# Gate and branch projections moved between the steps of a delta rule, and later DMA landings in a kernel's own planner

## The chip, the core and the metric

The kernel runs on one core of a Trainium2 chip. Its time is device microseconds of one execution, the median of several runs; less is better.

## What is computed

A sequence of 256 tokens with 1024 channels goes through two attention layers, a norm, and then twice through a "mixer" and a feed-forward network. The change lies in the mixer. Cut to what matters:

```
def hybrid_mixer(h, w_in, ...):
    proj = h @ w_in                       # 1024 x 7688
    (dn_qkv, dn_z, dn_b, dn_a, ret_q, ret_k, ret_v, ret_g, pool_u, gates) = split(proj)
    q, k, v = split(silu(causal_depthwise_conv(dn_qkv, dn_conv)))   # 4 taps, 4 heads of 128
    o_dn   = gated_delta_rule(l2(q), l2(k), v, sigmoid(dn_b), g)    # chunks of 64 tokens
    o_pool = multiscale_pool(pool_u, pool_w, pool_scale)
    o_ret  = chunkwise_retention(rotary(ret_q), rotary(ret_k), ret_v, ...)
    gt = sigmoid(gates).reshape(b, s, 3, 1024)
    y = (gt[:, :, 0] * (o_dn   @ w_branch_dn)
       + gt[:, :, 1] * (o_pool @ w_branch_pool)
       + gt[:, :, 2] * (o_ret  @ w_branch_ret))
    return y @ w_out
```

Inside the delta rule each chunk solves a triangular system (I + M) with M from k, the gates beta and the decays; the result feeds a state that is carried over four chunks of 64 tokens.

## The kernel before

Weights are read in float32. `piece` (two 128-row blocks of a weight matrix, up to 512 columns) issues one DMA into a `raw` tile on SP's queue, lets ScalarE cast it to `whi` and VectorE form the remainder `wlo`; there are 4 `raw`, 7 `whi` and 7 `wlo` buffers. `dense` then makes three matmuls for each block and each half of the tokens (whi and wlo against the two parts of the activations), into one of three `acc` PSUM tiles. So a product of 1024 x 512 weights is 4 pieces and 48 matmuls of 512 columns, one of 512 x 512 weights is 2 pieces and 24 matmuls.

A mixer (`mixer`) is written in this order. Retention comes first (its q, k, v and gate projections, its scores and its output `oT[4:8]`), then the pool (`oT[0:4]`), then `z0` (the delta rule's z, beta and a columns). From a come, in some twenty VectorE operations on 128x8 tiles, the log-decays `gg`; TensorE multiplies `gg` with four masks. Then come the decay masks `em` and `emT`, and `qkv(1, kTr)`: 96 matmuls of 256 columns and, on VectorE, two multiplications by `rr`, twelve convolution taps and two silu operations. Then M and `kn`, the solve of the 16x16 diagonal blocks (cN is moved by eight 8 KB DMAs to `Nb`, thirty small VectorE operations on `Tb`, eight DMAs back to `cT`), then `Tm` and `Sm`, `qkv(2, vT)`, `level(4)`, `qkv(0, qT)`, `level(5)`, the state over the four chunks, the normalised output `oTd`. Only behind all this stand, in the text, `gate` (the gates' columns, 1024 x 512 at a time, a tanh into a `tg` tile) and `branch` (512 x 512 at a time, its result times 1 + `tg` into `y`): pool in two halves, retention in two halves, then both gate halves of the delta rule, its branches and `w_out`.

The text's order is not the order on the engines. `Prog.record` writes down every operation with a cost and a priority (its place in the text), and `schedule` plays a machine through: each engine takes, of the operations that are ready, the one with the lowest place, and buffers of a class are handed out in the order of the text. What comes out is the fixed order of each engine's instructions; on the chip each engine then runs its list in order. When a DMA lands in this model is set by two lines:

```
hw = max(hw, t) + 460
dma = max(dma, hw + 840) + a.free() * a.shape[0] * 4 / 350.0
o.end = dma + 700
```

with a cost of 600 for loads that are broadcast over the partitions (`pv`, `gains`) and 380 for all others. `pv` (one buffer) holds small parameters; the mixer's first operation on VectorE halves 640 columns of it in place (`nrm`). Since `pv` comes free when the mixer before has used it last, the second mixer's `pv` is loaded, and halved, in the middle of the first mixer. In the trace every operation has line 389, the line of `emit` that issues it; tiles tell them apart (`b` and `s` are shared by many arrays, `m` and `ty` are the 128x8 ones, `kk` the constants, `st` the state).

Of the kernel before, what the change touches and what calls it, by code (L numbers as in the profile page):

```python
# [12 lines left out]
AF = mybir.ActivationFunctionType  # L13
ALU = mybir.AluOpType
AX = mybir.AxisListType

P = 128
S = 256
D = 1024
# [202 lines left out]
class Prog:  # L222
# [78 lines left out]
    def schedule(self):  # L301
        import heapq
        queue = {c: list(reversed(t)) for c, t in self.tiles.items()}
        free = {c: [(0.0, s) for s in range(v[0])] for c, v in self.classes.items()}
        waiting = {}
        for o in self.ops:
            o.wait += len(o.vts)
            for vt in o.vts:
                waiting.setdefault(id(vt), []).append(o)
        engines = ("PE", "DVE", "ACT", "POOL", "SP")  # L310
        now = {e: 0.0 for e in engines}
        pend = {e: [] for e in engines}
        avail = {e: [] for e in engines}
        dma = hw = 0.0
        held = {"DVE": 0.0, "POOL": 0.0}

        def release(o, t):
            o.ready = max(o.ready, t)
            o.wait -= 1
            if o.wait == 0:  # L320
                heapq.heappush(pend[o.eng], (o.ready, o.pri, id(o), o))

        def assign(c):
            while free[c] and queue[c]:
                vt = queue[c].pop()
                t, vt.slot = heapq.heappop(free[c])
                vt.avail = t
                for o in waiting.pop(id(vt), []):
                    release(o, t)
                if vt.left == 0:  # L330
                    heapq.heappush(free[c], (t, vt.slot))

        for c in self.classes:
            assign(c)
        order = []
        while len(order) < len(self.ops):
            best = None
            for e in engines:
                if avail[e] or pend[e]:
                    t = now[e] if avail[e] else max(now[e], pend[e][0][0])  # L340
                    if best is None or t < best[0]:
                        best = (t, e)
            if best is None:
                raise RuntimeError("the schedule is stuck: a class has too few slots")
            t, e = best
            while pend[e] and pend[e][0][0] <= t:
                _, p, i, o = heapq.heappop(pend[e])
                heapq.heappush(avail[e], (p, i, o))
            o = avail[e][0][2]
            if e in ("DVE", "ACT") and not o.crit:  # L350
                c = [q for q in pend[e] if q[3].crit and q[0] < t + 0.8 * o.cost and q[1] < o.pri]
                if c:
                    now[e] = min(c)[0]
                    continue
            heapq.heappop(avail[e])
            if self.shared(o):
                t = max(t, held["POOL" if e == "DVE" else "DVE"])
                held[e] = t + o.cost
            o.start = t
            now[e] = t + o.cost  # L360
            o.end = now[e]
            if e == "SP":
                a = (o.outs + o.ins)[0]
                hw = max(hw, t) + 460
                dma = max(dma, hw + 840) + a.free() * a.shape[0] * 4 / 350.0
                o.end = dma + 700
            order.append(o)
            for q in o.succ:
                release(q, o.end + LAT.get((e, q.eng), 100))
            for vt in o.vts:  # L370
                vt.left -= 1
                vt.last = max(vt.last, o.end)
                if vt.left == 0:
                    heapq.heappush(free[vt.cls], (vt.last + (230 if e == "PE" else 150), vt.slot))
                    assign(vt.cls)
        self.order = order
        self.span = max(o.end for o in order)
# [14 lines left out]
class Net:  # L392
# [541 lines left out]
    def mixer(self, l, xT, rx, nxt):  # L934
        nc = self.nc
# [2 lines left out]
        conv = pp[:, 0:48].rearrange("p (c k) -> p c k", k=4)  # L938
        psc, pw = pp[:, 48:52], pp[:, 52:564].rearrange("p (g d) -> p g d", g=4)
        nrm = pv[:, 8:648]  # L940
        nc.vector.tensor_scalar(nrm, nrm, 0.5, None, ALU.mult)
        dnn, retn = nrm[:, 0:128], nrm[:, 128:640]
        W = lambda *cols: self.chunk("w_in_2", l, list(cols))
        ts = lambda tt: slice(tt * P, tt * P + P)
        oT = self.new_xT()

        def plain(cols, fn):
            p = W(*cols)
            for tt in range(2):
                a = self.acc([P, sum(c[1] - c[0] for c in cols)])  # L950
                self.dense(a, xT, tt, p)
                fn(tt, a)
# [13 lines left out]
        def rot(tt, ps, dst):  # L966
            nat = self.s2([P, 4, P])
            self.rope(nat, ps.rearrange("p (h d) -> p h d", h=4), self.cosR, self.sinR, 4, P, tt, nc.vector, rx[tt][:, 0:1])
            pt = self.sd([P, 4, P])
            self.transposes(pt, nat.rearrange("p h d -> p (h d)"), 4)  # L970
            nc.scalar.copy(dst[:, :, ts(tt)], pt)
# [12 lines left out]
        a0 = self.acc([P, 512])  # L984
        self.dense(a0, xT, 1, pk)
        rot(1, a0, rkT)
        sc0 = self.b(9, [P, 4, S])
        sc1 = self.b(10, [P, 4, P])
        for h0 in (0, 2):
# [15 lines left out]
        for tt in range(2):  # L1005
# [14 lines left out]
            o = self.s2([P, 4, P])  # L1020
# [48 lines left out]
        a = sm()  # L1069
# [110 lines left out]
        kt = self.b(1, [P, 2, 4, P])  # L1180
        for tt in range(2):
            nc.vector.tensor_tensor(kt[:, tt], kn[:, tt], hd(tail, tt), ALU.mult)
        cp = self.b(0, [P, 832])
        cN, cT = (cp[:, i * P:i * P + P].rearrange("p (t h c) -> p t h c", t=2, h=4) for i in range(2))
        Nb, Tb = (cp[0:64, 320 + i * 256:576 + i * 256].rearrange("p (r c) -> p r c", r=16) for i in range(2))
# [13 lines left out]
        for tt in range(2):  # L1199
            for h in range(4):  # L1200
                nc.sync.dma_start(cT[:, tt, h], Tb[(tt * 4 + h) * 8:(tt * 4 + h) * 8 + 8])
        y = [self.b(12 + tt, [P, D]) for tt in range(2)]
        Tm, Sm = self.b(8, [P, 2, 4, P]), self.b(9, [P, 2, 4, P])
        for tt in range(2):
            nc.vector.tensor_tensor(Tm[:, tt].rearrange("p h (b c) -> p h b c", c=16),
# [5 lines left out]
        def level(lv):  # L1211
            for tt in range(2):
                ps = self.sd([P, 4, P])
                for h in range(4):
                    nc.tensor.matmul(ps[:, h], M[:, tt, h], Sm[:, tt, h], start=True, stop=True)
                wt = self.s2([P, 4, P])
                nc.vector.tensor_tensor(wt, ps, self.hb(self.masks[lv]), ALU.mult)
                ps = self.sd([P, 4, P])
                for h in range(4):
                    nc.tensor.matmul(ps[:, h], Tm[:, tt, h], wt[:, h], start=True, stop=True)  # L1220
                nc.vector.tensor_tensor(Sm[:, tt], Sm[:, tt], ps, ALU.subtract)
                if lv < 5:
                    nc.vector.transpose(Tm[:, tt].rearrange("p h d -> p (h d)"), Sm[:, tt].rearrange("p h d -> p (h d)"))

        qkv(2, vT)
        vb = self.b(5, [P, 2, 4, P])
        for tt in range(2):
# [2 lines left out]
        kb = self.b(2, [P, 2, 4, P])  # L1230
        for tt in range(2):
            nc.vector.tensor_tensor(kb[:, tt], kn[:, tt], hd(bGr, tt), ALU.mult)
        level(4)
        qkv(0, qT)
        rqs = []
# [4 lines left out]
        for tt in range(2):  # L1240
# [2 lines left out]
                nc.tensor.matmul(ps[:, h], kTr[:, h, ts(tt)], qT[:, h, ts(tt)], start=True, stop=True)  # L1243
            nc.vector.tensor_tensor(attnT[:, tt], ps, emT[:, tt], ALU.mult)
        level(5)
        uu, wq0, wq1 = self.b(10, [P, 2, 4, P]), self.b(3, [P, 4, P]), self.b(3, [P, 2, 4, P])
        wq = {(0, 1): wq0, (1, 0): wq1[:, 0], (1, 1): wq1[:, 1]}
        for tt in range(2):
# [12 lines left out]
        o = self.b(4, [P, 2, 4, P])  # L1261
# [41 lines left out]
            self.transposes(pt, of, 4)  # L1303
            self.split(oTd[0][:, :, ts(tt)], oTd[1][:, :, ts(tt)], pt)

        def gate(bi, h):
            tg = []

            def fn(tt, a):
                t = nc.tile("tg", [P, 512])  # L1310
                nc.scalar.activation(t, a, AF.Tanh, scale=rx[tt][:, 1:2])
                tg.append(t)
            plain([(4616 + bi * D + h * 512, 4616 + bi * D + h * 512 + 512)], fn)
            return tg

        def branch(name, h, src, k0, tg, first):
            s = slice(h * 512, h * 512 + 512)
            p = self.chunk(name, l, [(h * 512, h * 512 + 512)], 4)
            for tt in range(2):
                a = self.acc([P, 512])  # L1320
                self.dense(a, src, tt, p, k0)
                if first:
                    nc.vector.scalar_tensor_tensor(y[tt][:, s], tg[tt], 1.0, a, ALU.add, ALU.mult)
                else:
                    nc.vector.scalar_tensor_tensor(tg[tt], tg[tt], 1.0, a, ALU.add, ALU.mult)
                    nc.vector.tensor_tensor(y[tt][:, s], y[tt][:, s], tg[tt], ALU.add)

        for h in range(2):
            branch("w_branch_pool_2", h, oT, 0, gate(1, h), True)
        for h in range(2):  # L1330
            branch("w_branch_ret_2", h, oT, 4, gate(2, h), False)
        tgs = [gate(0, h) for h in range(2)]
        yT = self.new_xT()
        for h in range(2):
# [146 lines left out]
```

## Time and profile before

| | us |
|---|---|
| median of 3 runs (1206.88 to 1207.74) | 1206.95 |
| profiled execution, its own time | 1212.46 |
| its span, first to last instruction | 1210.7 |
| TensorE busy in the span | 1182.1 |
| mean granted TensorE clock | 0.993 of full speed |

The profile adds up busy time per engine; an engine's idle time before an instruction is listed with what ended it. "PE" is TensorE, "DVE" VectorE, "ACT" ScalarE, "SPq" the queue that issues the DMAs. Mixer 0 ends some way into the span (about 230 to 545 us), mixer 1 runs from about 725 to 1015 us; their delta rules begin near 334 and 808 us.

### The profile page before, as it was taken

The numbers are of one execution on the slowest core, as the hardware profiler recorded it, in microseconds if no ns is written. First come the engines' busy times: TensorE is split into PE (matmuls) and PEld (weight loads), VectorE is DVE, ScalarE is ACT, GpSimd is POOL, SyncE is SP. The second block draws the span as 40 slices with busy tenths as digits, with TensorE's granted clock in tenths as the row PEclk, the third lists the DMA queues.
The fourth block names the chain that finished last, engine by engine and source line by source line (L and its number), as shares of the span: only waits on it lengthen the run. The fifth ranks groups of instructions, "written<-read, shape, count | busy, mean of one in ns | idle before, by whom it ended". The sixth has DMA issues, their size and how long they took to land.

```text
span 1210.7 us, 17627 instructions
## 1 busy us (share of the span) xinstructions
PE 1182.1 (98%) x6468; PEld 1002.0 (83%) x6468; DVE 878.7 (73%) x1584; ACT 644.1 (53%) x1196; POOL 48.4 (4%) x65
## 2 busy tenths in 40 slices
PE   8999999999989999999999999999899999999997
PEld 6898889888889788887888888899788888788886
DVE  7988789887679877677655638679977866655643
ACT  6687568855345444555544536445454545544431
POOL 0100110000001001000000001000000001000000
PEclk9999999999989999999999999999999999999999
DMA  7354435545461763546554864544374454664661
GB/s 252 111 162 118 144 106 191 182 147 176 123 203 54 214 216 105 174 124 219 170 184 134 266 208 139 166 136 153 111 241 136 143 192 126 205 206 135 203 204 36
DMA packets 64664, 197.10 MB, mean 163 GB/s; under 512 B 11200, under 2 KB 12608, under 8 KB 64576
## 3 DMA queue, kind: packets, MB, share of 16 engines
q1 hardware_dynamic: 64576, 195.96, 50.3%
q8 instruction: 51, 0.84, 0.3%
q14 instruction: 37, 0.30, 0.1%
HBM read 194.62 MB, written 1.05 MB: 162 GB/s over the span
## 4 chain that ended last, share of the span: by engine, by line
PE 80%; DVE 10%; DMA 5%; ACT 3%; issue 2%; POOL 0%; SPq 0%; POOLq 0%; ACTq 0%; DVEq 0%
PE acc L389 63%; PE sd L389 17%; DVE s L389 3%; DMA raw<-in_wt 3%; DVE wlo L389 3%; DVE b L389 2%; ACT whi L389 1%; DMA pv<-in_pv 1%; ACT b L389 1%; DMA raw<-in_wc 1%; DVE ty L389 1%; POOL ty L389 0%; DVE tg L389 0%; DMA gc<-in_gcol 0%; SPq L389 0%
## 5 line engine op out<-in xcount | busy, mean ns | idle before, releaser
L389 DVE TENSOR_TENSOR wlo<-raw,whi 128x1024 fp32r<-128x1024 f32 (+4 forms) x380 | 428.7, 1136 | 145.7 <-ACT whi L389 143.4
L389 ACT CAST whi<-raw 128x1024 fp32r<-128x1024 f32 (+4 forms) x380 | 370.3, 982 | 237.8 <-PE acc L389 144.5
L389 PE MATMUL acc<-whi,xh 128*128 128x512 f32 (+4 forms) x1184 | 446.2, 378 | 5.7 <-ACT whi L389 2.4
L389 PE MATMUL acc<-wlo,xh 128*128 128x512 f32 (+4 forms) x1184 | 444.2, 376 | 6.0 <-DVE wlo L389 6.0
L389 PE MATMUL acc<-whi,xl 128*128 128x512 f32 (+4 forms) x1184 | 444.3, 376 | 0.0
L389 PEld LDWEIGHTS acc<-wlo,xh 128*128 128x128 f32 x1184 | 223.7, 189 | 46.4 <-DVE wlo L389 8.4
L389 PEld LDWEIGHTS acc<-whi,xh 128*128 128x128 f32 x1184 | 223.1, 189 | 45.8 <-ACT whi L389 3.5
L389 PEld LDWEIGHTS acc<-whi,xl 128*128 128x128 f32 x1184 | 223.6, 189 | 37.7 <-DVE xl L389 0.3
L389 PE MATMUL acc<-whi,b 128*128 128x512 f32 x328 | 107.1, 396 | 0.0
L389 PE MATMUL sd<-b,b 128*128 128x128 f32 (+3 forms) x496 | 74.8, 291 | 0.3 <-ACT b L389 0.2
L389 PEld LDWEIGHTS acc<-whi,b 128*128 128x128 f32 x328 | 61.5, 188 | 14.1
L389 PEld LDWEIGHTS sd<-b,b 128*128 128x128 f32 (+2 forms) x496 | 65.1, 191 | 6.5 <-DVE b L389 2.0
L389 POOL TENSOR_TENSOR ty<-ty,m 128x4 f32<-128x4 f32 (+3 forms) x34 | 33.7, 993 | 878.5 <-DVE ty L389 878.5
L389 PE MATMUL acc<-wlo,b 128*128 128x512 f32 x164 | 64.7, 395 | 0.0
L389 ACT ACTIVATE b<-sd 128x512 fp32r<-128x512 f32 (+3 forms) x44 | 23.4, 537 | 60.1 <-PE sd L389 57.9
L389 PE MATMUL acc<-xh,wlo 128*128 128x256 f32 x192 | 55.1, 287 | 0.0
L389 PE MATMUL acc<-xh,whi 128*128 128x256 f32 x192 | 54.7, 286 | 0.0
L389 PE MATMUL acc<-xl,whi 128*128 128x256 f32 x192 | 54.6, 285 | 0.0
L389 ACT ACTIVATE s<-acc,r 128x512 f32<-128x512 f32 (+3 forms) x52 | 31.2, 600 | 43.1 <-PE acc L389 40.3
L389 PE MATMUL sd<-c,s 128*128 128x128 f32 (+2 forms) x260 | 40.1, 274 | 1.7 <-DVE s L389 1.5
L389 DVE SCALAR_TENSOR_TENSOR b<-sd,b 128x512 fp32r<-128x512 f32 (+3 forms) x44 | 26.7, 615 | 18.1 <-ACT b L389 17.2
L389 PEld LDWEIGHTS sd<-c,s 128*128 128x128 f32 (+2 forms) x260 | 30.7, 138 | 9.8 <-DVE s L389 3.2
(172 smaller groups left out, 1274.7 us busy)
## 6 DMA issues: line engine op xcount, KB each, us to landing
raw<-in_wt SPq DMA_DIRECT2D x308, 512.0 KB
raw<-in_wt SPq DMA_DIRECT2D x40, 256.0 KB
raw<-in_wt SPq DMA_DIRECT2D x16, 384.0 KB
raw<-in_wt SPq DMA_DIRECT2D x8, 352.0 KB
b<-in_gains SPq DMA_DIRECT2D x5, 512.0 KB
raw<-in_wt SPq DMA_DIRECT2D x8, 264.0 KB
b<-in_kd SPq DMA_DIRECT2D x2, 512.0 KB
b<-in_kp SPq DMA_DIRECT2D x2, 512.0 KB
```

Source lines behind the costliest of these rows:

```text
L389: o.inst = getattr(eng[o.eng], o.name)(*[real(a) for a in o.args], **{k: real(v) for k, v in o.kw.items()})
```

## The change

Three edits. The planner lets a DMA land later: 1500 after its transfer instead of 700, and 3500 for those with a cost over 500 (the broadcast ones). The halving of `nrm` moves in the text from the mixer's start to behind the fourth rotation of retention. And `gate` and `branch`, unchanged, are defined and called earlier: each of the four pool and retention halves (gate, then branch) gets its own place in the delta rule: ahead of the 16x16 solve, ahead of `qkv(2)`, ahead of `level(4)` and behind `level(5)`. `y` is allocated ahead of the solve.

```diff
-                o.end = dma + 700
+                o.end = dma + (3500 if o.cost > 500 else 1500)
...
         nrm = pv[:, 8:648]
-        nc.vector.tensor_scalar(nrm, nrm, 0.5, None, ALU.mult)
...
         rot(1, a0, rkT)
+        nc.vector.tensor_scalar(nrm, nrm, 0.5, None, ALU.mult)
         sc0 = self.b(9, [P, 4, S])
...
             nc.vector.tensor_tensor(kt[:, tt], kn[:, tt], hd(tail, tt), ALU.mult)
+        def gate(bi, h):
+            tg = []
+
+            def fn(tt, a):
+                t = nc.tile("tg", [P, 512])
+                nc.scalar.activation(t, a, AF.Tanh, scale=rx[tt][:, 1:2])
+                tg.append(t)
+            plain([(4616 + bi * D + h * 512, 4616 + bi * D + h * 512 + 512)], fn)
+            return tg
+
+        def branch(name, h, src, k0, tg, first):
+            s = slice(h * 512, h * 512 + 512)
+            p = self.chunk(name, l, [(h * 512, h * 512 + 512)], 4)
+            for tt in range(2):
+                a = self.acc([P, 512])
+                self.dense(a, src, tt, p, k0)
+                if first:
+                    nc.vector.scalar_tensor_tensor(y[tt][:, s], tg[tt], 1.0, a, ALU.add, ALU.mult)
+                else:
+                    nc.vector.scalar_tensor_tensor(tg[tt], tg[tt], 1.0, a, ALU.add, ALU.mult)
+                    nc.vector.tensor_tensor(y[tt][:, s], y[tt][:, s], tg[tt], ALU.add)
+
+        y = [self.b(12 + tt, [P, D]) for tt in range(2)]
+        branch("w_branch_pool_2", 0, oT, 0, gate(1, 0), True)
         cp = self.b(0, [P, 832])
...
-        y = [self.b(12 + tt, [P, D]) for tt in range(2)]
         Tm, Sm = self.b(8, [P, 2, 4, P]), self.b(9, [P, 2, 4, P])
...
+        branch("w_branch_pool_2", 1, oT, 0, gate(1, 1), True)
         qkv(2, vT)
...
             nc.vector.tensor_tensor(kb[:, tt], kn[:, tt], hd(bGr, tt), ALU.mult)
+        branch("w_branch_ret_2", 0, oT, 4, gate(2, 0), False)
         level(4)
         qkv(0, qT)
...
         level(5)
+        branch("w_branch_ret_2", 1, oT, 4, gate(2, 1), False)
         uu, wq0, wq1 = self.b(10, [P, 2, 4, P]), self.b(3, [P, 4, P]), self.b(3, [P, 2, 4, P])
...
-        for h in range(2):
-            branch("w_branch_pool_2", h, oT, 0, gate(1, h), True)
-        for h in range(2):
-            branch("w_branch_ret_2", h, oT, 4, gate(2, h), False)
         tgs = [gate(0, h) for h in range(2)]
```

(The old definitions of `gate` and `branch`, word for word the same, go.)

## Rows read from the trace of the kernel before

**Rows 1.** Busy time of each stage: engine, busy us, (instructions), PE clock, DMA share.

```profile
330.00:545.00 215.00, 207.54 (x1189) 179.98 (x1189) 168.11 (x308) 107.28 (x192) 9.29 (x13) 0.98 0.50 157
545.00:805.00 260.00, 259.45 (x1237) 213.41 (x1236) 162.69 (x238) 123.46 (x177) 7.52 (x8) 1.00 0.55 181
805.00:1020.00 215.00, 209.74 (x1211) 180.92 (x1210) 172.67 (x321) 111.41 (x204) 10.21 (x15) 0.99 0.50 159
```

**Rows 2.** Timeline of TensorE, those after an idle time: mixer 0, then mixer 1.

```profile
357.03 1.24 PE L389 MATMUL sd<-m,kk 128*128 128x8 f32 x5 [3.65 <-DVE m L389]
...
392.80 0.50 PE L389 MATMUL acc<-whi,xh 128*128 128x512 f32 x1 [1.29 <-DVE s L389]
...
398.63 0.50 PE L389 MATMUL acc<-wlo,xh 128*128 128x512 f32 x1 [0.48 <-DVE wlo L389]
...
403.71 0.50 PE L389 MATMUL acc<-wlo,xh 128*128 128x512 f32 x1 [2.03 <-DVE wlo L389]
...
827.91 1.06 PE L389 MATMUL sd<-m,kk 128*128 128x8 f32 x8 [1.52 <-DVE m L389]
...
861.50 0.50 PE L389 MATMUL acc<-whi,xh 128*128 128x512 f32 x1 [0.82 <-DVE s L389]
...
867.33 0.50 PE L389 MATMUL acc<-wlo,xh 128*128 128x512 f32 x1 [0.45 <-DVE wlo L389]
...
872.40 0.77 PE L389 MATMUL acc<-wlo,xh 128*128 128x512 f32 x1 [2.00 <-DVE wlo L389]
```

**Rows 3.** The same columns as rows 1, for stretches of the delta rules.

```profile
356.00:364.00 8.00, 6.97 (x30) 6.68 (x31) 6.25 (x15) 2.69 (x5) 0.00 (x0) 0.57 0.47 151
404.00:410.00 6.00, 6.00 (x20) 4.71 (x20) 4.29 (x5) 2.60 (x4) 0.00 (x0) 0.72 0.89 252
872.00:876.00 4.00, 3.60 (x9) 2.87 (x10) 4.00 (x5) 1.56 (x2) 0.00 (x0) 0.57 0.60 160
828.00:832.00 4.00, 3.89 (x29) 3.56 (x30) 3.94 (x8) 1.23 (x3) 0.00 (x0) 1.00 0.73 225
360.00:404.00 44.00, 40.19 (x280) 36.94 (x280) 41.73 (x89) 21.44 (x47) 3.62 (x6) 0.96 0.25 75
404.00:450.00 46.00, 46.00 (x193) 37.05 (x193) 35.00 (x61) 22.87 (x25) 0.00 (x0) 0.96 0.77 245
```

**Rows 4.** Timeline of VectorE and of SP's queue around the load of `pv`.

```profile
347.62 0.68 SPq L389 DMA_DIRECT2D pv<-in_pv  x1
...
354.19 0.49 DVE L389 TENSOR_SCALAR pv<-pv 128x640 f32<-128x640 f32 x1 [2.69 <-DMA pv<-in_pv]
```

**Rows 5.** VectorE from 361 to 404 us by operation and shape: busy us, mean ns.

```profile
L389 DVE TENSOR_TENSOR wlo<-raw,whi 128x1024 fp32r<-128x1024 f32 x6 | 7.4, 1229 | 0.2 <-ACT whi L389 0.2
L389 DVE SCALAR_TENSOR_TENSOR s<-s,pp,s 128x254 f32<-128x254 f32 x12 | 5.4, 487 | 0.0
...
L389 DVE SCALAR_TENSOR_TENSOR b<-s,s 128x512 f32<-128x512 f32 x6 | 4.2, 702 | 0.0
L389 DVE TENSOR_TENSOR s<-acc,rr 128x512 f32<-128x512 f32 x6 | 4.2, 692 | 1.5 <-PE acc L389 1.5
```

**Rows 6.** VectorE from 404 to 450 us, the same.

```profile
L389 DVE TENSOR_TENSOR wlo<-raw,whi 128x1024 fp32r<-128x1024 f32 x21 | 25.4, 1222 | 9.5 <-ACT whi L389 9.5
```

**Rows 7.** The chain that ended last: matmuls of 256 and of 512 columns.

```profile
364.60 10.61 PE acc L389 x90
...
570.94 15.82 PE acc L389 x68
```

**Rows 8.** ScalarE and VectorE, timeline: `oTd`'s last part, and the last tanh of a gate.

```profile
494.69 0.68 DVE L389 TENSOR_TENSOR b<-sd,b 128x512 fp32r<-128x512 f32 x1
...
508.20 0.69 ACT L389 ACTIVATE tg<-acc,r 128x512 f32<-128x512 f32 x1 [0.35 <-PE acc L389]
```

**Rows 9.** A weight load on SP's queue and the ScalarE cast that waits for it.

```profile
351.25 0.33 SPq L389 DMA_DIRECT2D raw<-in_wt  x1
...
355.56 1.04 ACT L389 CAST whi<-raw 128x1024 fp32r<-128x1024 f32 x1 [3.15 <-DMA raw<-in_wt]
```

More of the change, by code (lines that the diff above doesn't have):

```diff
@@ L1304, in mixer @@
             self.split(oTd[0][:, :, ts(tt)], oTd[1][:, :, ts(tt)], pt)
[L1306 to L1326, printed above, removed]
-        for h in range(2):
-            branch("w_branch_pool_2", h, oT, 0, gate(1, h), True)
-        for h in range(2):
-            branch("w_branch_ret_2", h, oT, 4, gate(2, h), False)
         tgs = [gate(0, h) for h in range(2)]
```

## The prediction, on record before the changed kernel was seen

> **What bounds the kernel now.** I read the busy times by stage first, then TensorE's idle times, then what the engine that ends them was doing. TensorE works 1182.1 of 1210.7 us, so no order of the same work can save more than the 28.6 us of idle time and what a lowered clock costs. In the stretch from 545 to 805 us it is idle for 0.55 of 260 us; the two stretches with the delta rules lose 7.46 and 5.26 us, at mean clocks of 0.98 and 0.99 [rows 1]. The change has to earn its time there.
>
> The idle times there are few [rows 2], and of two kinds. One stands ahead of the product of `gg` with the masks (3.65 us in mixer 0, 1.52 in mixer 1): TensorE has this product next in its list and waits for VectorE's chain of 128x8 operations. In mixer 0 that chain is held up by something foreign to it: the halving of the next mixer's `pv` stands in VectorE's list, and VectorE sat 2.69 us until the load had landed, 354.19 - 347.62 = 6.57 us after its issue [rows 4]. The planner's lines give this load 460 + 840 + 948 + 700 = 2.95 us, so it put the operation where VectorE had to wait. The second kind, 1.29 + 0.48 + 2.03 us in mixer 0 and 0.82 + 0.45 + 2.00 in mixer 1, is a wait for VectorE's ordinary work, a weight remainder or an `acc` not yet read out [rows 2]. From 360 to 404 us VectorE is busy 41.73 of 44 us, from 404 to 450 us only 35.00 of 46 [rows 3]: full while the three projections of q, k, v come one behind the other, and with 11.0 us to spare while the gates run.
>
> Each kind also costs clock. After the 3.65 us the granted clock was 0.57 on average over 356 to 364 us, after the 2.03 us it was 0.72 over 404 to 410, after the 2.00 us 0.57 over 872 to 876; after the lone 1.52 us it stayed at 1.00 [rows 3]. It is the lower of its two levels (1.2 of 2.4 GHz) for part of each stretch, so the matmuls there ran at half rate; what that loses is the length times one minus the mean: 3.44, 1.68 and 1.72 us.
>
> **The later landings.** Their certain effect is at `pv`: the model now holds it back for 460 + 840 + 948 + 3500 = 5.75 us, 2.8 us later than before, and the wait to be removed is 2.69 us. So the halving slips behind about as much VectorE work as it waited, and mixer 0's gap should shrink to that of mixer 1: 3.65 - 1.52 = 2.13 us, and the clock lost behind it, 3.44 us, since the same gap of 1.52 us lost none. That is 5.57 us. Late next is the chain of `gg` itself, in both mixers the same 1.52 us; I leave it. Moving the halving in the text does little by itself: one 640-column operation a mixer, and the case that hurts is run a mixer ahead, as whatever VectorE has nothing better to do than.
>
> The DMA page of the Trainium skill ("DMA: Bandwidth & Descriptors", Anatomy of one DMA; its fit is for GpSimd's queue) puts a load at about 2.0 us and its bytes at 436 GB/s, an estimate of 2.8 us for the 324 KB of `pv`. By that the old constant would have been right and the new one 3 us too careful, and this term would be 0 instead of 5.57. This trace measured 6.57 us, and the measurement decides.
>
> For the weights the model moves by 0.8 us, from 460 + 840 + 1498 + 700 = 3.50 to 4.30 us. One that ScalarE waited for came 355.56 - 351.25 = 4.31 us after its issue [rows 9], so the new figure is the nearer one. What it does to the order elsewhere the trace cannot show. Bounds: it can gain little where 0.55 of 260 us is idle [rows 1]; it loses nothing as long as casts are ahead, which seven buffers at 12 matmuls of 15.82/68 = 0.233 us each (2.8 us a piece, 19.5 us in hand) [rows 7] make likely, and 0.8 us at each of the handful of stage starts where they are not, some 4 us. I take a loss of 1 us.
>
> **The moved gates and branches.** No work is added or removed: each of the four sets a mixer (a gate half and a branch half) has 6 pieces, so 6 loads on SP's queue, 6 casts, 6 remainders, 72 matmuls and two tanh operations. Its TensorE time is 72 x 0.233 = 16.7 us [rows 7]. Its VectorE time is 6 x 1.222 = 7.3 us [rows 6] and, at 0.70 us for a 128x512 operation [rows 5], 1.4 us for the pool or 2.8 for retention: 8.7 to 10.1 us, 52 to 60% of TensorE's. A projection of q, k or v is the other way round: TensorE 96 x 10.61/90 = 11.3 us [rows 7]; VectorE four remainders, 4.9 us, a third of the taps (three groups of 12 like the one shown, 16.2 us in all), of the silu and of the `rr` operations (4.2 us each), 8.2 us [rows 5]: 13.1 us, 116%. Three in a row ask VectorE for 39 us in TensorE's 34, with the masks and M on top; that is why it saturates. With a set between each two, the mix falls below one: from 360 to 450 us VectorE has 41.73 + 35.00 = 76.7 us of work, against TensorE's 40.19 + 46.00 less the 1.68 us of lost clock, 84.5 us. VectorE is then 91% full and no longer the bound.
>
> So the gaps of the second kind, 3.80 and 3.27 us, and the clock lost behind them, 1.68 and 1.72, are to be had: 10.47 us. With only 7.8 us of VectorE's time left free in 84.5, in fixed lists, where it also waits for ScalarE's casts (9.5 us from 404 to 450 [rows 6]), I do not expect all of it: bounds are 0 (the saturation only moves) and all 10.47, and I take three quarters, 7.9 us.
>
> The clock page ("TensorE: Matmul & The Clock Gate", HAM oscillation and the second failure mode behind it) says in the Trainium skill that short idles between groups of matmuls, repeated, lower the clock too. The three gaps of 3.80 us together agree, the lone 1.52 us does not. By this rule a residue of small gaps would keep the 3.40 us of lost clock, and the sum would be some 2.5 us less.
>
> What else moves: the 24 loads of the sets now stand on SP's queue ahead of and among the sixteen 8 KB moves of the solve, each held until a `raw` buffer is free; and on VectorE the solve's small operations now come behind the remainders of the first set, 8.7 us. Both delay the chain from the solve by the levels and the state to `oTd`. Nothing waits for that chain but the last branches, and gates cover it: in mixer 0 `oTd` is complete at 495.4 us, while gates last until their last tanh at 508.2 [rows 8], 12.8 us later. Less the 5.48 us that TensorE will be quicker before it, 7.3 us of cover stay. POOL gets nothing new. `y` holds two `b` buffers no longer than before, as it already stood between `cp` and `Tm`.
>
> **The sum.** 5.57 + 7.9 - 1.0 = 12.4 us. Against the profiled execution's own 1212.46 us that gives 1200.0. The median of the runs shown is 5.5 us lower, at 1206.95, and the same difference makes it 1194.5 us. A measurement of this kernel can tell about 0.2%, 2.4 us, from no change.
>
> **The rivals.** (a) VectorE stays the bound: the masks, the convolution of k and M still come at once, and a convolution now meets the solve. For it speaks the 91%; against it the 11.0 us free beside the gates. Then only 5.57 us come, 1201.4. (b) The new order gives back elsewhere what it earns: casts ordered later at the stage starts (4 us) and the old gaps at new places; 1206 to 1207. For it speaks that one constant redraws every list; against it the casts in hand. (c) Slower: the chain to `oTd` outlasts the gates. Ahead of it in VectorE's list now stand up to three sets, 8.7 + 8.7 + 10.1 = 27.5 us, where none stood; every microsecond beyond the cover of 7.3 is idle TensorE time, in each mixer. It eats the 16.0 us of possible gain when the chain is 7.3 + 8.0 = 15.3 us late in each, and with all 27.5 us the kernel loses 2 x 20.2 - 16.0 = 24 us, 1231. Against it: the two convolutions that stood ahead of the solve's end (2 x 13.1 us) now come later.
>
> **How the numbers follow.** Forecast 0.68, (a) 0.14, (b) 0.08, (c) 0.10. The likeliest case alone runs from all gaps of both kinds gone (16.0 us and the two 1.52, so 19 us: 1188) to about half of the second kind, 1199. To hold eight in ten the range takes in (a) as well, 1188 to 1203. Faster by over 0.2% are the forecast and (a), 0.82; within 0.2% is (b), 0.08; slower is (c), 0.10.
>
> **What would show it.** Right: no wait of VectorE for `pv`; the gap ahead of the `gg` product near 1.5 us in both mixers, at full clock behind it; between 360 and 450 us VectorE's busy share even, near 90%, and TensorE's gaps of the second kind below 1 us a mixer; the tanh rows spread over that stretch. Wrong: gaps of TensorE for `wlo` or `acc` of the old size at new places (a), idle time at the stage starts (b), or idle time between the last tanh and the product with `oTd` (c).

## The result, and the profile after

The changed kernel takes 1194.61 us (median of 4 runs, 1192.61 to 1197.78) where the kernel before took 1206.91 in the runs beside it (4): 0.9899 of its time, with a 95% interval of 0.9877 to 0.9921. Forecast were 1194.5 us. The total is right; two of its three terms are not. Their errors cancel only in part, and some 4 us come from nothing that the forecast names, so that the total came out as it did is luck.

The profiled execution took 1197.78 us with a span of 1196.0, so 14.7 us less than the profiled one before (spans, 1210.7 - 1196.0). The page's line for TensorE:

```profile
PE 1175.1 (98%) x6468; PEld 999.8 (84%) x6468; DVE 878.6 (73%) x1584; ACT 643.5 (54%) x1196; POOL 47.2 (4%) x65
```

Idle time fell from 28.6 to 1196.0 - 1175.1 = 20.9 us, which is 7.7; the other 7.0 us are busy time, 1182.1 - 1175.1: the same 6468 matmuls ran that much quicker. By stage, with the columns of [rows 1] (engine busy, clock, DMA share), and the stretches that the prediction spoke of:

```profile
0.00:60.00 60.00, 53.30 (x321) 44.47 (x322) 50.11 (x134) 41.38 (x100) 7.95 (x13) 1.00 0.56 183
60.00:330.00 270.00, 267.03 (x1661) 232.45 (x1660) 224.06 (x470) 181.78 (x433) 11.30 (x14) 1.00 0.47 148
330.00:545.00 215.00, 212.67 (x1225) 184.95 (x1224) 173.93 (x324) 113.63 (x208) 10.34 (x15) 0.98 0.51 165
545.00:805.00 260.00, 260.00 (x1268) 216.15 (x1267) 161.46 (x233) 123.42 (x170) 5.60 (x7) 1.00 0.55 178
805.00:1020.00 215.00, 213.30 (x1210) 183.09 (x1209) 176.34 (x325) 112.38 (x202) 10.87 (x15) 1.00 0.53 167
...
360.00:450.00 90.00, 89.79 (x497) 77.73 (x497) 76.75 (x147) 47.67 (x75) 3.09 (x6) 0.99 0.52 167
404.00:450.00 46.00, 46.00 (x279) 40.82 (x278) 38.87 (x82) 23.64 (x31) 0.00 (x0) 1.00 0.58 179
355.00:363.00 8.00, 7.21 (x30) 6.82 (x31) 6.09 (x12) 2.33 (x5) 0.00 (x0) 0.57 0.53 189
819.00:827.00 8.00, 7.68 (x45) 6.71 (x46) 7.87 (x16) 4.68 (x10) 0.00 (x0) 1.00 0.42 135
```

The two delta rule stages lose 2.33 and 1.70 us instead of 7.46 and 5.26 [rows 1]. VectorE's third column shows why: 76.75 us of work from 360 to 450 us, the 76.7 us forecast, but 38.87 of them now fall in the second half of that stretch, where it had 35.00 [rows 3]; TensorE is idle for 0.21 us in all 90. What is left in these two stages of idle times above 0.4 us stands in three rows of TensorE's timeline (the first of mixer 0, the others of mixer 1):

```profile
355.79 1.87 PE L389 MATMUL sd<-m,kk 128*128 128x8 f32 x8 [2.01 <-DVE m L389]
...
819.32 1.06 PE L389 MATMUL sd<-m,kk 128*128 128x8 f32 x8 [1.17 <-DVE m L389]
835.54 0.71 PE L389 MATMUL sd<-b 128*128 128x128 f32 x4 [0.46 <-DVE b L389]
```

Of the waits for `wlo` and `acc` [rows 2] none is left. The gap ahead of the `gg` product is still there: 2.01 us, and behind it the clock was at 0.57 for 355 to 363 us, the same 8 x 0.43 = 3.44 us lost as before [rows 3]. VectorE's timeline says that it still waits for `pv`, now 1.16 us instead of 2.69 [rows 4]; the first row is SP's issue of the load, 6.74 us ahead of the halving:

```profile
348.42 0.94 SPq L389 DMA_DIRECT2D pv<-in_pv  x1
...
355.16 0.49 DVE L389 TENSOR_SCALAR pv<-pv 128x640 f32<-128x640 f32 x1 [1.16 <-DMA pv<-in_pv]
```

And the cover of [rows 8] is gone: `oTd`'s last split now begins 4.08 us after the last tanh of a gate does (505.05 - 500.97), where it had ended 12.8 us ahead of it. It costs nothing only because the branch of the first 128 tokens needs the first split alone, which is done at 497.2 (VectorE, ScalarE):

```profile
496.52 0.69 DVE L389 TENSOR_TENSOR b<-sd,b 128x512 fp32r<-128x512 f32 x1 [1.65 <-ACT b L389]
505.05 0.69 DVE L389 TENSOR_TENSOR b<-sd,b 128x512 fp32r<-128x512 f32 x1 [0.45 <-ACT b L389]
...
500.97 0.69 ACT L389 ACTIVATE tg<-acc,r 128x512 f32<-128x512 f32 x1 [0.34 <-PE acc L389]
```

### The profile page after: what moved, and what is told of

Read it like the earlier page. It is cut to its first block, busy times and chain, and to the rows that moved or that the text cites. A ratio compares the mean times of both kernels' runs of the same rounds, so it can differ in the third digit from the quotient of the medians.

```text
span 1196.0 us, 17636 instructions
## 1 busy us (share of the span) xinstructions
PE 1175.1 (98%) x6468; PEld 999.8 (84%) x6468; DVE 878.6 (73%) x1584; ACT 643.5 (54%) x1196; POOL 47.2 (4%) x65
## 4 chain that ended last, share of the span: by engine, by line
PE 89%; DVE 4%; DMA 4%; ACT 2%; issue 1%; SPq 0%; POOLq 0%; DVEq 0%; ACTq 0%
PE acc L389 71%; PE sd L389 18%; DMA raw<-in_wt 2%; DVE s L389 1%; DVE b L389 1%; DMA kk<-in_k 1%; DVE wlo L389 1%; ACT whi L389 1%; ACT b L389 1%; DMA pv<-in_pv 1%; SPq L389 0%; DVE ty L389 0%; ACT s L389 0%; DVE tg L389 0%; DVE m L389 0%
## 5 line engine op out<-in xcount | busy, mean ns | idle before, releaser
L389 PEld LDWEIGHTS acc<-xh,wlo 128*128 128x128 f32 x192 | 37.3, 194 | 0.3
```

Source lines behind the costliest of these rows:

```text
L389: o.inst = getattr(eng[o.eng], o.name)(*[real(a) for a in o.args], **{k: real(v) for k, v in o.kw.items()})
```

## The experiments

Theory 1 is the prediction's: three projections of q, k and v in a row ask more of VectorE than TensorE's time, and the moved sets (a gate half and a branch half each) relieve it. The rival is that one edit alone, the landing constants with the lists they redraw, brings the gain. The kernels came in three groups, each on a chip with runs of the kernel before beside them (medians 1207.34, 1207.7 and 1206.58); a ratio is against those runs.

**The sets alone.** The changed kernel with the old landing and the halving back at the mixer's start.

```diff
-                o.end = dma + (3500 if o.cost > 500 else 1500)
+                o.end = dma + 700
...
         nrm = pv[:, 8:648]
+        nc.vector.tensor_scalar(nrm, nrm, 0.5, None, ALU.mult)
...
-        nc.vector.tensor_scalar(nrm, nrm, 0.5, None, ALU.mult)
```

> Only the four sets of gates and branches are moved; the landing stays at 700 and the halving of nrm at the mixer's start. Theory 1 (the sets take VectorE's saturation away, a gain of its own): TensorE's waits for wlo and acc between 388 and 404 us and between 858 and 873 us (3.80 and 3.27 us before) are gone, the wait of VectorE for pv (2.69 us) and the 3.65 us gap stay; 1197 to 1200 us. Theory 2 (the gain comes from a truer landing in the model, the sets are reshuffled work): the waits for wlo and acc stay, 1204 us or more.

Measured: 1196.63 us, 0.9908 (0.9872 to 0.9944), just under the 1197 to 1200 expected. No wait for `wlo` or `acc` over 0.4 us is left in either mixer, so the sets remove the second kind of gap by themselves. Not expected was that the `gg` gap shrank as well, to 1.37 us in mixer 0, at full clock, and to under 0.3 in mixer 1:

```profile
354.85 1.06 PE L389 MATMUL sd<-m,kk 128*128 128x8 f32 x8 [1.37 <-DVE m L389]
```

The clock behind it, as in [rows 3]:

```profile
354.00:362.00 8.00, 7.10 (x41) 6.18 (x42) 7.78 (x17) 5.79 (x11) 0.00 (x0) 1.00 0.59 203
```

VectorE waits only 0.73 us for `pv` here: the load, issued at 347.40, was there at 352.01, after 4.61 us.

**The landings alone.** The kernel before with the new landing line and the halving moved; gates and branches stay behind the delta rule.

```diff
-                o.end = dma + 700
+                o.end = dma + (3500 if o.cost > 500 else 1500)
...
         nrm = pv[:, 8:648]
-        nc.vector.tensor_scalar(nrm, nrm, 0.5, None, ALU.mult)
...
+        nc.vector.tensor_scalar(nrm, nrm, 0.5, None, ALU.mult)
```

> The text's order of the kernel before, with the later landings and the moved halving only. Theory 1: the waits for wlo and acc stay at 3 to 4 us a mixer with their clock loss, and only the gap ahead of the product with gg shrinks, by the 1.5 us that VectorE's wait for pv became shorter in the changed kernel; 1203 to 1206 us. Theory 2: most of the gain is here, 1197 to 1200 us.

Measured: 1203.33 us, 0.9966 (0.9945 to 0.9987), so 4 us. The second kind of gap stands where it stood, 3.69 us in mixer 0 and 3.35 in mixer 1 (the three waits of mixer 0):

```profile
389.56 0.50 PE L389 MATMUL acc<-whi,xh 128*128 128x512 f32 x1 [1.13 <-DVE s L389]
395.39 0.50 PE L389 MATMUL acc<-wlo,xh 128*128 128x512 f32 x1 [0.51 <-DVE wlo L389]
400.43 0.56 PE L389 MATMUL acc<-wlo,xh 128*128 128x512 f32 x1 [2.05 <-DVE wlo L389]
```

Its clock went with it; the columns are those of [rows 3], the first row for the `gg` gap of mixer 0, the others behind the waits for `wlo` in mixers 0 and 1:

```profile
354.00:362.00 8.00, 7.17 (x44) 6.90 (x45) 6.87 (x17) 3.51 (x7) 0.00 (x0) 0.79 0.57 204
400.00:408.00 8.00, 7.57 (x26) 6.07 (x27) 5.14 (x7) 3.94 (x5) 0.00 (x0) 0.79 0.84 256
867.00:875.00 8.00, 7.15 (x24) 5.71 (x25) 5.13 (x6) 3.68 (x5) 0.00 (x0) 0.79 0.72 238
```

The rival falls: alone, the sets bring some 11 us of the 12, the landings (with the moved halving, which was not run apart) some 4, and together they bring less than the sum. What the landings add to the sets is not shown: the changed kernel's 0.9899 lies within the interval of the 0.9908 without them. And the `gg` gap behind which the first row shows a lowered clock was of 1.37 us, the very length that lost nothing in the kernel with the sets alone.

**`pv` really held back.** The step that failed at once was the planner's: `cost` looks for a broadcast among the inputs of an operation, but a load's source in HBM is not recorded as an input, so no load ever costs 600, and the 3500 is never taken. (What was said of this cost ahead of the prediction is wrong for this reason.) Any other figure in place of 3500 would give the same lists. So `pv` got 1500 like all others, 0.8 us more and not 2.8. Here it gets the 3500:

```diff
-            return 600.0 if any(p[0] == "partition_broadcast" for a in o.ins for p in a.ops) else 380.0
+            return 600.0 if o.outs and o.outs[0].vt.cls == "pv" else 380.0
```

> The changed kernel, but the planner's cost of 600 is given to the loads of pv by name. In the kernel before and in the changed one the condition looks for a broadcast among the operation's recorded inputs, and a load's source in memory is not recorded there, so that no load has the cost of 600 and the 3500 is never used; here pv gets it, 2.0 us more. Theory 1: VectorE's wait for pv (1.16 us in the changed kernel) is gone, TensorE's gap ahead of the product with gg in mixer 0 falls from 2.01 to about 1 us; with it the clock stays up behind it (3.4 us), 1190 to 1192 us. Rival: the clock falls behind a gap of 1 us as well and only the 1.2 us come, 1193 to 1194 us; or the wait was not what held the chain, 1194 to 1195 us.

Measured: 1192.34 us, 0.9868 (0.9836 to 0.9899). VectorE no longer waits for `pv`, and the `gg` gap is 0.23 us in mixer 0 and 0.58 in mixer 1, so the mechanism is as the prediction had it. Its size was then taken again, beside the changed kernel itself:

> The version with pv held back once more, beside the changed kernel. If holding pv back is worth what the profile showed (the gap of 2.01 us ahead of the product with gg down to 0.2), it stays 1.5 us and more ahead of the changed kernel, up to 4 us where the clock falls less often; if it was the chip, the two are within 1 us.

> The changed kernel itself once more, on the same chip as the next two, so that differences of 2 us among them can be told from those between chips: 1192 to 1197 us.

Measured: 1192.75 us, 0.9876 (0.9855 to 0.9897), for `pv` held back, and 1193.53, 0.9883 (0.9861 to 0.9904), for the changed kernel. The 0.8 us between them cannot be told from nothing; this is the quickest version seen, and not shown to beat the changed one.

The profile of this second run of the changed kernel, with the same lists, shows how much of the reading of `pv` is one execution's. VectorE waited for TensorE earlier in its list and then found `pv` landed, 6.24 us after its issue; the `gg` gap of mixer 0 was 1.24 us instead of 2.01, and the clock behind it stayed up. Mixer 1's gap was 1.50 us instead of 1.17, and there the clock fell (the gaps, then the clock in the same order):

```profile
355.67 1.06 PE L389 MATMUL sd<-m,kk 128*128 128x8 f32 x8 [1.24 <-DVE m L389]
...
817.00 1.06 PE L389 MATMUL sd<-m,kk 128*128 128x8 f32 x8 [1.50 <-DVE m L389]
```

```profile
355.00:363.00 8.00, 7.33 (x42) 6.17 (x43) 7.87 (x16) 4.84 (x10) 0.00 (x0) 1.00 0.56 196
816.00:824.00 8.00, 7.00 (x37) 6.49 (x38) 7.18 (x16) 3.74 (x8) 0.00 (x0) 0.79 0.52 174
```

**Only `pv` held back.** The kernel with `pv` held back, with 700 in place of 1500 for every other load.

```diff
-                o.end = dma + (3500 if o.cost > 500 else 1500)
+                o.end = dma + (3500 if o.cost > 500 else 700)
```

> The four sets moved and pv held back (3500, by name); all other loads at the old 700. Theory: for the weights the later landing is worth nothing where seven buffers are in hand, so this equals the version with pv held back within 1.5 us. Rival: the truer landing of the weights is worth 2 us and more of its own, and this one is that much slower.

Measured: 1201.97 us, 0.9959 (0.9942 to 0.9975): missed by some 9 us, on the rival's side. The mixers are nearly as good as in the others (`gg` gaps of 1.29 and 1.40 us, 1.7 us of clock lost in mixer 1, no wait for `wlo` or `acc`). The largest part of the loss lies in the first layer. The stretch from 0 to 60 us, first here, then in the kernel with the sets alone (columns of [rows 1]):

```profile
0.00:60.00 60.00, 50.88 (x267) 42.00 (x268) 45.76 (x124) 38.24 (x89) 8.98 (x13) 0.91 0.57 189
```

```profile
0.00:60.00 60.00, 54.13 (x319) 44.75 (x319) 49.66 (x133) 41.30 (x99) 6.96 (x13) 1.00 0.56 183
```

TensorE is idle for 3.25 us more, the longest wait being one of 2.17 us for ScalarE at 47.3 us, and up to 0.09 x 60 = 5.4 us of clock are lost. (With `pv` held back and weights at 1500, on the same chip, TensorE is busy for 53.79 us there at a clock of 0.97.) The attention layers load a `pv` too, so this constant redraws their lists as well; which operation it moved to its harm, and why it hurts with weights at 700 and not with weights at 1500, is not shown. It shows rival (b) at work: a constant meant for one place redraws all lists.

**Is it VectorE's load?** The kernel before, in its old order, with two of the four convolution taps left out.

```diff
-                for t in (2, 1, 0):
+                for t in (2,):
```

> The kernel before, in its own order, with two of the convolution's four taps left out (the planner makes its lists anew): 24 of the 36 tap operations in each mixer are gone from VectorE, some 10.8 us at 0.45 us each. Theory 1 (VectorE's load, and nothing else, makes TensorE's waits for wlo and acc): without any set moved, these waits fall below 1 us in each mixer, from 3.80 and 3.27; 1197 to 1202 us. Rival (the order itself or the number of acc and weight buffers makes them): they stay at 3 us, 1204 us or more.

Measured: 1197.49 us, 0.9906 (0.988 to 0.9932). The edit takes 8 of the 12 tap operations from each projection, 8 x 0.487 = 3.9 us [rows 5], so that its 13.1 us on VectorE become 9.2, below TensorE's 11.3. All waits for `wlo` and `acc` are gone without any set being moved; from 360 to 404 us TensorE is idle for 0.34 us, and VectorE busy for 38.65 us instead of 41.73 [rows 3]:

```profile
360.00:404.00 44.00, 43.66 (x295) 39.94 (x294) 38.65 (x70) 27.48 (x53) 3.18 (x6) 1.00 0.52 162
```

What decides these waits is on which side of TensorE's time VectorE's comes out, and either way of getting there gives nearly the same gain (0.9906 and 0.9908). Not all of it is VectorE's: the `gg` gap shrank here too, from 3.65 and 1.52 us to 1.65 and 0.95.

**Half the sets.** The changed kernel with the two retention sets put back behind `oTd`.

```diff
-        branch("w_branch_ret_2", 0, oT, 4, gate(2, 0), False)
...
-        branch("w_branch_ret_2", 1, oT, 4, gate(2, 1), False)
...
+        for h in range(2):
+            branch("w_branch_ret_2", h, oT, 4, gate(2, h), False)
         tgs = [gate(0, h) for h in range(2)]
```

> The changed kernel with the two pool sets in their new places, the two retention sets back behind the delta rule. The projections of v and q then come one behind the other. Theory 1 in its simple form (VectorE's load per stretch decides, and 26 us of VectorE against 23 us of TensorE is covered by the seven weight buffers): within 2 us of the changed kernel, 1193 to 1197 us, and the chain to oTd ends earlier against the last gate, since fewer sets stand ahead of it. Rival (each pair of projections needs a set between): waits for wlo or acc of 1.5 us and more a mixer return, 1197 to 1201 us.

Measured: 1204.42 us, 0.997 (0.9951 to 0.999). Both expectations missed. The waits for `wlo` and `acc` are gone with two sets too, so VectorE is relieved; but now TensorE waits for `oTd` in both mixers, which is the prediction's rival (c):

```profile
502.34 0.63 PE L389 MATMUL sd<-c,b 128*128 128x128 f32 x4 [2.54 <-DVE b L389]
503.64 0.62 PE L389 MATMUL acc<-whi,b 128*128 128x512 f32 x1 [0.68 <-ACT b L389]
```

These are mixer 0's; mixer 1 has the same two waits, 2.53 and 0.68 us. The clock behind each pair:

```profile
502.00:510.00 8.00, 6.99 (x27) 5.52 (x28) 5.24 (x11) 1.71 (x8) 1.01 (x1) 0.79 0.32 119
968.00:976.00 8.00, 7.26 (x21) 5.60 (x22) 4.07 (x9) 1.47 (x7) 1.01 (x1) 0.57 0.29 100
```

3.22 and 3.21 us idle, and up to 8 x 0.21 + 8 x 0.43 = 5.1 us of clock. `oTd`'s last split begins at 510.74 us, 10.9 us after the last tanh. What had made the chain late shows on SP's queue: the second eight of the small moves (`b<-b`) go out almost all one at a time, because the model holds each until it thinks the one before has landed and puts weight loads between them; on the chip those loads wait for a `raw` buffer, 16.3 us in all for `wlo` between 425 and 462 us. The first and the last of the moves:

```profile
436.07 0.70 SPq L389 DMA_DIRECT2D b<-b  x1
...
458.81 0.63 SPq L389 DMA_DIRECT2D b<-b  x1
```

**Half the sets, without that queue.** The moves do not depend on one another: behind a rearrange, the slices of cN and cT keep the box of the whole array in the planner, so each seems to overlap the one before. Here each slice is cut before the rearrange and has its own box.

```diff
-        cN, cT = (cp[:, i * P:i * P + P].rearrange("p (t h c) -> p t h c", t=2, h=4) for i in range(2))
+        cN = [cp[:, t * 64:t * 64 + 64].rearrange("p (h c) -> p h c", h=4) for t in range(2)]
+        cT = [cp[:, P + t * 64:P + t * 64 + 64].rearrange("p (h c) -> p h c", h=4) for t in range(2)]
...
-                nc.sync.dma_start(cT[:, tt, h], Tb[(tt * 4 + h) * 8:(tt * 4 + h) * 8 + 8])
+                nc.sync.dma_start(cp[:, P + tt * 64 + h * 16:P + tt * 64 + h * 16 + 16], rowb(1, tt * 4 + h))
```

> The kernel with only the pool sets moved, and the solve's sixteen small moves written so that the planner sees the columns and rows that each one touches; before, each was recorded as touching the whole of its array, so that the planner held every move back until the one ahead had landed. Theory: the moves held up the chain to oTd (spread over 23.4 us each way in that kernel, 14.6 us in the kernel before), and TensorE's wait of 2.5 + 0.7 us for oTd in each mixer is the chain's lateness; here the moves go out in 6 us, the wait is gone and the clock stays up behind it: 1195 to 1199 us. Rival (the chain is late on VectorE or behind the sets on TensorE): the wait stays, 1202 to 1205 us.

Measured: 1197.55 us, 0.991 (0.9887 to 0.9932), 7 us quicker than with the queue. The moves go out eight at a time (SP), `oTd`'s last split begins 30 us before the last tanh (VectorE, ScalarE), and no wait for it is left in either mixer (one of 1.10 us for an `acc` is back in mixer 0):

```profile
385.10 5.50 SPq L389 DMA_DIRECT2D b<-b  x8
406.71 5.29 SPq L389 DMA_DIRECT2D b<-b  x8
```

```profile
470.77 0.68 DVE L389 TENSOR_TENSOR b<-sd,b 128x512 fp32r<-128x512 f32 x1
...
500.88 0.69 ACT L389 ACTIVATE tg<-acc,r 128x512 f32<-128x512 f32 x1 [0.34 <-PE acc L389]
```

**All of it together.** `pv` held back, all four sets, own boxes.

> The changed kernel with pv held back, and the same own boxes for the sixteen moves. TensorE waited for no part of the chain there, so by the theory nothing is to be gained in time: within 2 us of the kernel with pv held back, 1190 to 1194 us, while oTd is complete 10 us and more earlier and gates are left behind it. Rival: an earlier chain lets level and state steps fall among the sets and helps or hurts: beyond 3 us either way.

Measured: 1196.72 us, 0.9902 (0.9882 to 0.9922): missed by some 3 us, and not better than without the boxes. `oTd`'s last split begins 4.4 us ahead of the last tanh, where it began 4.1 us behind it with `pv` held back alone. With all four sets moved nothing waits for `oTd` anyway, so the earlier chain has nothing to give. What the redrawn lists lose was found only in part: TensorE has a wait of 1.27 us for VectorE in mixer 1 that the second run of `pv` held back has not; mixer 0 has small gaps of 1.09 and 0.64 us, but that second run has nearly the same (0.74 and 0.63) and took 1192.75 us.

**The cover taken away.** The changed kernel with the delta rule's own two gate halves ahead of the state as well, so that no gate is left to run beside it.

```diff
+        tgs = [gate(0, h) for h in range(2)]
...
-        tgs = [gate(0, h) for h in range(2)]
```

> The changed kernel with the two gate halves of the delta rule, the last work that can fill TensorE's time while the state goes over its four chunks, placed ahead of the state in the text. Theory 1 (the chain to oTd needs gates beside it; rival c of the prediction): TensorE goes idle between the steps of the state, 10 to 17 us in each mixer (some 72 matmuls of 0.23 us stood there), and the clock falls: 1212 to 1235 us. Rival: the planner lets the state's steps through as early as they are ready and the chain is short: within 3 us of the changed kernel, 1192 to 1198 us.

Measured: 1217.01 us, 1.0075 (1.005 to 1.01), so 22 us slower than the changed kernel. The steps of the state now wait for each other, 6.0 us in each mixer where 10 to 17 were expected (three of seven rows of mixer 1):

```profile
960.80 4.07 PE L389 MATMUL sd<-b,b 64*128 64x128 f32 x16 [0.78 <-DVE b L389]
967.35 2.07 PE L389 MATMUL sd<-b,b 64*128 64x128 f32 x8 [0.77 <-DVE b L389]
...
976.67 1.08 PE L389 MATMUL sd<-c,b 128*128 128x128 f32 x4 [1.48 <-DVE b L389]
```

The clock there, first of mixer 0, then of mixer 1:

```profile
485.00:510.00 25.00, 18.97 (x104) 15.84 (x103) 14.86 (x28) 5.80 (x23) 2.02 (x2) 0.80 0.25 95
958.00:985.00 27.00, 20.97 (x87) 17.61 (x86) 14.27 (x27) 4.65 (x19) 2.02 (x2) 0.62 0.18 62
```

The clock costs about as much as the waits, which are 12.1 us: over TensorE's busy time it is 18.97 x 0.20 + 20.97 x 0.38 = 11.8 us. What two gate halves hide is worth more than all that the change gains.

## Why the prediction was right, and where it was not

- **VectorE's saturation** was the right reading of [rows 3]: the sets alone remove the gaps, and so does taking work from VectorE with no set moved. The work from 360 to 450 us came out as forecast, 76.75 us for 76.7.
- **The term of 7.9 us was too small.** "I do not expect all of it" and three quarters of 10.47 was the step that failed. In both profiles of the changed kernel all of 3.80 and 3.27 us went, and both clock falls behind them (3.40 us): 10.47 us. (The 0.46 us left in mixer 1 is another wait, which was 0.35 us before.) At 91% VectorE was not the bound at all, in spite of fixed lists and casts.
- **The term of 5.57 us for `pv` was too large.** "The model now holds it back for 5.75 us" took a special case of the planner as given that is never reached. In the first profile the gap went from 3.65 to 2.01 us, 1.64 of the 2.13 us forecast, and the 3.44 us of clock behind it stayed. In the second it went to 1.24 us, at full clock as forecast, while mixer 1 lost 1.7 us of clock: 2.41 + 3.44 - 1.7 = 4.2 us. With the hold made real VectorE's wait is gone in both its profiles (gaps of 0.23 and 0.74 us) and the clock stays up behind, but the median moved by 0.8 us only beside the changed kernel on one chip. The 3.65 us themselves were read in one profile; in no other on record, old landing or new, is mixer 0's gap over 2.09 us.
- **"The same gap of 1.52 us lost none"** was one execution's reading. A gap of 1.37 us lost nothing with the sets alone and 1.68 us (8 x 0.21) with the landings alone. With two sets put back a gap of 2.09 us lost none, in the changed kernel one of 2.01 us lost 3.44. So a clock fall cannot be booked to one gap of 1 to 2 us; the prediction's sum did so for 3.44 us. (Its reckoning, length times one minus the mean, also counts the waits in a stretch; over the busy time alone these are 6.97 x 0.43 = 3.0 us.) The rule weighed there, of the Trainium skill ("TensorE: Matmul & The Clock Gate", A second HAM failure mode: psum-queue depth-cycling), is that short idles between groups of matmuls, often enough, make the clock fall and rise again. The kernel without cover agrees: gaps of 0.7 to 1.5 us, seven to a mixer, and 3.8 and 8.0 us lost to the clock.
- **The loss of 1 us at the landings** is not shown. In the first profile it fits: TensorE's idle time rose from 6.36 to 6.70 us in the first 60 us, and from 1.94 to 2.97 us between 60 and 330, where no gate was moved: 1.4 us. In the second profile these stretches lose 4.68 and 3.44 us, 8.1 us together against 8.3 before. The load from which the prediction took 4.30 us as the nearer figure was read wrongly [rows 9]: by the semaphore that it waits for, the cast at 355.56 us waits for the load issued at 348.82, 6.74 us earlier; the one issued at 351.25 landed at 357.99. Both figures of the planner are too short there.
- **The cover of 7.3 us was wrong.** Forecast was that `oTd` stays that far ahead of the last tanh; it fell 4.08 us behind. Beside the sets ahead of it in VectorE's list, the later landings stretch the sixteen small moves, which the model strings one behind the other: the second eight took 14.6 us on SP before and 20.6 after. (With the sets alone they took 15.6 us, and the last split was done 3.8 us ahead of the last tanh.) Rival (c) was nearer than its chance of 0.10 said; with two sets put back its wait came true, though not its loss against the kernel before.
- **The sum**: 1.64 + 10.47 - 1.4 = 10.7 us by these terms in the profiled pair, where the spans differ by 14.7 and the medians by 12.3. Of the 4.0 us left, mixer 1's `gg` gap (1.52 to 1.17) and the stretch from 545 to 805 us (0.55 to 0) give 0.9, and other small idle times take back 0.5. The rest is busy time of TensorE: of the 7.0 us that its matmuls became shorter, the clock in the mixers explains 3.4 (three falls before, one after), which the 10.47 hold already. The other 3.6 us have no cause that was shown. They do not come with the sets alone: less its clock falls, TensorE is busy for 1175.3 us in the kernel before and 1175.1 with the sets alone, but 1171.7 in the changed kernel and 1172.7 with the landings alone. The kernel with fewer taps, at the old landing, lies between (1173.8), so the landings are not shown to be the cause either. That terms so far off add up to 12.4 us, where 12.3 were measured, is luck; that the waits for VectorE would go is not.

## What to carry to other kernels

Look at the busy share of the next engine stretch by stretch: an engine at 73% over the span can be the bound where three heavy stages follow one another, and a light stage placed between them relieves it at no cost, as long as something is left to run beside the serial chain behind. Before pricing a change of a planner's constant, make sure that the case it names is ever reached; and a constant that holds one thing in one place redraws every list, so price it over the whole span. Work moved forward as filler is taken from the cover of whatever comes last: measure what that cover still hides. And read a gap or a clock fall from more than one execution before a term of a forecast rests on it.

## What the runs showed of the chip

The time from the issue of the `pv` load to the first operation that needed it was 6.57 and 6.74 us in the kernels before and after, 4.61 with the sets alone, where VectorE waited for it each time: the same 324 KB on the same queue, with other loads around it. The first mixer's load of the same size took 3.25 us from issue to landing in the kernel before, the second's 6.55; weight loads of 512 KB issued between 337 and 352 us took 3.4 to 6.7 us. The estimate of 2.8 us from the Trainium skill ("DMA: Bandwidth & Descriptors", Anatomy of one DMA) is not far under the 3.25 us and far under the others; its fit is for GpSimd's queue. And the clock differs from one execution of the same kernel to the next: in 23 executions of the kernel before on one chip the mean granted clock was 0.989 to 0.998, the times 1203.7 to 1216.2 us, and an execution at 0.991 (1212.70 us) against one at 0.998 (1203.76) differs by 8.9 us, where 0.007 of the span is 8.4. This is most of the spread of these runs, and over two thirds of the 12.3 us that the change gains.
